# Mixture-of-experts stage of a two-layer trunk: first two narrow expert blocks taken whole, with twelve weight loads queued ahead of the register loads

## Chip, core and metric

The kernel runs on one core of a Trainium2 chip. The metric is the device time of one execution in microseconds, smaller is better; the time of a kernel is the median of its runs.

## What is computed

The reference is a two-layer trunk on 256 tokens of width 1024. Each layer adds a mixing block (a recurrent group, an attention group and a gated group) and a feed-forward block. The feed-forward block is dense in layer 0 and a top-2-of-8 mixture of experts in layer 1. The change lies in this last part:

```
def moe_swiglu(h, router, wg, wu, wd):          # h: (1, 256, 1024) float32
    t = h.reshape(256, 1024)
    logits = (t @ router).astype(float32)         # 8 experts
    top_v, top_i = lax.top_k(logits, 2)
    gates = softmax(top_v)
    gate_full = sum(one_hot(top_i, 8) * gates[..., None], axis=1)
    out = 0
    for e in range(8):                            # wg, wu: 1024x3584, wd: 3584x1024 each
        out = out + gate_full[:, e:e+1] * ((silu(t @ wg[e]) * (t @ wu[e])) @ wd[e])
    return out
```

The weights of the eight experts are 8 x 42 pieces of 1 MB in float32, 336 loads in all, and every one of them is read.

## The kernel before

**Places.** The kernel serves the experts in eight places. Place 0 is always expert 0, whose number is known when the program is built; the other seven are filled by the number of tokens, and their expert numbers are worked out on the chip (tile `order`) and read into registers of the DMA-issuing engine SP. Places 1, 2 and 3 are WIDE (128 token columns; place 1 carries a QUARTER piece of 32 more), places 4 to 6 are NARROW (64) and places 0 and 7 are QUARTER (32). For every place the tokens are gathered by matmuls with a one-hot matrix (`prepare`, L1250 for the narrow places, L1264 for the wide ones), evacuated by ACT and DVE into `xgs` or `xg`.

**Blocks.** An expert is worked in 7 blocks of 512 hidden columns. A block takes 6 loads: j = 0 to 3 (gate and up weights) and j = 4, 5 (down weights). A narrow block multiplies the float32 weights as they are: `small_up` (L1486 for a QUARTER, L1470 for a NARROW), then a transpose (L1510, copied by ACT at L1513) and `small_down` (L1539). A wide block first splits every half of a load into a high part (`wh`, ACT, L196) and a low part (`wl`, DVE, L197) and uses three matmuls for each product (L201 to L203); at place 1 the same loads then serve `quarter_up` (L1486), which is the last reader of j = 0 to 3.

**What sets the order.** `work` goes through the wide blocks. In every turn it does the up part of one wide block, the down part of the wide block before, the down parts of the narrow blocks taken up in the turn before, and the up parts of two more (or one). Before its first turn it does `small_up` of the first LEAD = 2 narrow blocks, both of expert 0. `halves` hands out the loads in that order, `take` pulls one half and refills the queue `feed` with `fill` (window of 10 halves, 3 of them split). The order on each engine is then set by a scheduler when the program is built; `tc.issue_after(i)` puts an instruction behind `i` on the engine of `i`.

**Buffers.** Expert loads go in a ring of 12 buffers of 1 MB: 8 of pool `raw2` and 4 of pool `raw`. Load n + 12 can be issued when the last reader of load n is done. Before the experts, `raw2` holds the work area of the mixing block and `raw` the last weights of that block (w_out).

**Number the loads from 0.** Before: 0 to 7 are j = 0 to 3 of the two lead blocks; 8 to 11 are j = 0 to 3 of the first wide block (place 1, so behind a register); 12 to 15 are j = 4, 5 of the lead blocks; 16 to 23 are j = 0 to 3 of the next two narrow blocks (expert 0 too); 24 to 27 the second wide block.

## Time and profile before

| | us |
|---|---|
| median of 3 runs (lowest to highest) | 1416.84 (1415.02 to 1419.85) |
| the profiled execution, its own time | 1414.25 |
| its span (first to last instruction) | 1412.50 |
| experts: from the first expert matmuls at 553.8 to the end | 859 |
| mean granted TensorE clock over the span, share of full speed | 0.97 |

The span is cut in stretches: layer 0 and the mixing block of layer 1 fill the first 540 us, the routing of the experts some 15 us behind them, and the experts the rest. In the last part TensorE and the DMA engines are both nearly always busy, so the busy shares alone don't say which of them sets the pace; the chain of waits does.

### The profile page before, as it was taken

The numbers are of one execution on the slowest core, as the hardware profiler recorded it, in microseconds if no ns is written. First come the engines' busy times: TensorE is split into PE (matmuls) and PEld (weight loads), VectorE is DVE, ScalarE is ACT, GpSimd is POOL, SyncE is SP. The second block draws the span as 40 slices with busy tenths as digits, with TensorE's granted clock in tenths as the row PEclk, the third lists the DMA queues.
The fourth block names the chain that finished last, engine by engine and source line by source line (L and its number), as shares of the span: only waits on it lengthen the run. The fifth ranks groups of instructions, "written<-read, shape, count | busy, mean of one in ns | idle before, by whom it ended". The sixth has DMA issues, their size and how long they took to land.

```text
span 1412.5 us, 24089 instructions
## 1 busy us (share of the span) xinstructions
PE 1330.2 (94%) x9860; PEld 965.4 (68%) x9860; DVE 715.0 (51%) x1052; ACT 629.0 (45%) x986; POOL 77.9 (6%) x127
## 2 busy tenths in 40 slices
PE   7989899999999898998999999999999999999986
PEld 7977678888888676765666555655766656656553
DVE  5686455445576555453335314524544446565443
ACT  7548264444575643453224313423434345444342
POOL 1250000000114111000000000000000000000000
PEclk9989999999999997999999999999999999999989
DMA  7410245555452231899999999989999999999995
GB/s 285 178 61 2 90 153 185 189 188 179 159 185 74 84 159 71 337 425 425 425 427 425 426 385 374 426 372 426 402 426 413 420 427 426 426 411 426 427 426 226
DMA packets 60438, 422.64 MB, mean 299 GB/s; under 512 B 7200, under 2 KB 8224, under 8 KB 10400
## 3 DMA queue, kind: packets, MB, share of 16 engines
q1 hardware_dynamic: 59760, 420.03, 73.1%
q8 instruction: 79, 1.29, 0.3%
q10 hardware_dynamic: 560, 1.00, 0.2%
q14 instruction: 39, 0.32, 0.1%
HBM read 419.95 MB, written 1.05 MB: 298 GB/s over the span
## 4 chain that ended last, share of the span: by engine, by line
PE 76%; DMA 10%; DVE 6%; ACT 3%; POOL 2%; issue 2%; SPq 0%; ACTq 0%; DVEq 0%; POOLq 0%
PE pb L1470 10%; DMA raw<-moe 10%; PE pb L202 8%; PE pb L201 7%; PE pb L203 7%; PE pa L1539 7%; PE pa L202 6%; PE pa L201 6%; PE pa L203 6%; PE pb L1486 4%; DVE wl L197 2%; PE pb L1250 1%; PE pa L371 1%; PE pa L373 1%; PE pa L372 1%
## 5 line engine op out<-in xcount | busy, mean ns | idle before, releaser
L197 DVE TENSOR_TENSOR wl<-raw,wh 128x1024 fp32r<-128x1024 f32 (+1 forms) x370 | 440.8, 1221 | 180.1 <-ACT wh L196 179.4
L196 ACT ACTIVATE wh<-raw 128x1024 fp32r<-128x1024 f32 (+1 forms) x370 | 380.5, 1053 | 230.8 <-PE pb L203 118.4
L202 PE MATMUL pb<-wl,xg 128*128 128x512 f32 x336 | 141.3, 420 | 13.2 <-DVE wl L197 12.4
L1470 PE MATMUL pb<-raw,xgs 128*64 128x256 f32 x1344 | 151.0, 380 | 0.0
L201 PE MATMUL pb<-wh,xg 128*128 128x512 f32 x336 | 136.7, 409 | 9.9 <-ACT wh L196 9.9
L203 PE MATMUL pb<-wh,xg 128*128 128x512 f32 x336 | 134.0, 399 | 0.0
L1470 PEld LDWEIGHTS pb<-raw,xgs 128*64 128x64 f32 x1344 | 95.0, 137 | 54.7 <-issue 9.3
L1539 PE MATMUL pa<-raw,aT 128*32 128x256 f32 (+1 forms) x1008 | 120.1, 454 | 0.0
L1486 PE MATMUL pb<-raw,xgs 128*32 128x256 f32 x1344 | 93.1, 395 | 10.1 <-DMA raw<-moe 10.1
L202 PEld LDWEIGHTS pb<-wl,xg 128*128 128x128 f32 x336 | 64.4, 192 | 41.9 <-DVE wl L197 25.9
L1473 ACT ACTIVATE a<-pb,rg 128x256 f32<-128x256 f32 x21 | 9.9, 473 | 174.9 <-PE pb L1470 174.9
L1501 DVE TENSOR_TENSOR aT<-pb,aT 128x512 fp32r<-128x512 f32 x21 | 14.5, 692 | 143.7 <-ACT aT L1500 143.7
L201 PEld LDWEIGHTS pb<-wh,xg 128*128 128x128 f32 x336 | 64.2, 191 | 32.1 <-ACT wh L196 18.2
L1539 PEld LDWEIGHTS pa<-raw,aT 128*32 128x32 f32 (+1 forms) x1008 | 42.8, 118 | 61.9 <-issue 46.2
L1486 PEld LDWEIGHTS pb<-raw,xgs 128*32 128x32 f32 x1344 | 45.2, 113 | 50.9 <-DMA raw<-moe 14.1
L202 PE MATMUL pb<-wl,hTh 128*128 128x512 f32 (+1 forms) x192 | 73.0, 380 | 0.0
L203 PEld LDWEIGHTS pb<-wh,xg 128*128 128x128 f32 x336 | 64.5, 192 | 12.1
L203 PE MATMUL pb<-wh,hTl 128*128 128x512 f32 (+1 forms) x192 | 71.6, 377 | 0.0
L202 PE MATMUL pa<-wl,aT 128*128 128x512 f32 x168 | 69.0, 411 | 0.5 <-DVE wl L197 0.5
L201 PE MATMUL pb<-wh,hTh 128*128 128x512 f32 (+1 forms) x192 | 67.5, 378 | 0.7 <-ACT hTh L284 0.7
L203 PE MATMUL pa<-wh,aT 128*128 128x512 f32 x168 | 66.5, 396 | 0.0
L1475 DVE SCALAR_TENSOR_TENSOR a<-pb,rg,a 128x256 f32<-128x256 f32 x21 | 10.2, 484 | 99.4 <-PE pb L1470 99.4
(384 smaller groups left out, 2058.0 us busy)
## 6 DMA issues: line engine op xcount, KB each, us to landing
raw<-moe SPq DMA_DIRECT2D x336, 1024.0 KB, 12.3
raw<-wst SPq DMA_DIRECT2D x54, 1024.0 KB, 4.8
raw<-wst SPq DMA_DIRECT2D x4, 832.0 KB, 5.1
area<-sw_in SPq DMA_DIRECT2D x2, 960.0 KB, 7.1
area<-sw_in SPq DMA_DIRECT2D x2, 664.0 KB, 6.2
x<-x_in SPq DMA_DIRECT2D x2, 512.0 KB, 5.1
raw<-wst SPq DMA_DIRECT2D x2, 512.0 KB, 7.0
out_dram<-x SPq DMA_DIRECT2D x8, 128.0 KB, 2.7
```

The costliest lines, as they stand in the source:

```text
L196: act(h[:, 0:n], t[:, a:b], AF.Copy)
L197: (E or V).tensor_tensor(lo[:, 0:n], t[:, a:b], h[:, 0:n].bitcast(F32), op=ALU.subtract)
L201: T.matmul(o, lhsT=xh, rhs=wh, start=first, stop=False)
L202: T.matmul(o, lhsT=xh, rhs=wl, start=False, stop=False)
L203: T.matmul(o, lhsT=xl, rhs=wh, start=False, stop=last)
L371: T.matmul(ps, lhsT=wh[:, s_], rhs=hTh[:, k, :], start=(k == 0), stop=False)
L372: T.matmul(ps, lhsT=wh[:, s_], rhs=hTl[:, k, :], start=False, stop=False)
L373: T.matmul(ps, lhsT=wl[:, s_], rhs=hTh[:, k, :], start=False, stop=(k == KD - 1))
L1470: T.matmul(ps[HALF[hv], :], lhsT=z[:, k, :], rhs=w[:, o_:o_ + 256], start=(k == 0), stop=(k == KD - 1))
L1486: T.matmul(ps[QUART[g], :], lhsT=z[:, k, :], rhs=ws[g // 2 * 4 + k // 2][:, o_:o_ + 256], start=(k == 0), stop=(k == KD - 1))
L1501: V.tensor_tensor(z[:, :, 1, :], p3, z[:, :, 0, :].bitcast(F32), op=ALU.subtract)
L1539: T.matmul(acc[rows, :], lhsT=aT[:, f, :], rhs=ws[f][:, g * w:g * w + w], start=(i == 0 and f == 0), stop=(i == NB - 1 and f == 3))
```

## The change

- The order in which the loads are handed out: all six loads of the two lead blocks come first (j = 0 to 3 of both, then j = 4, 5 of both), and twelve loads instead of ten halves are queued before the first register is needed. While this stock lasts, `take` refills nothing.
- The two lead blocks are done whole, up and down, before the first wide turn; their `small_down` is taken out of the first turn.
- The first six splits of the first wide block are put behind the copies of the transposed activations of the two lead blocks (`last_a`) and behind the last gather copy of the wide place (`gathered`).
- The low part `xl` of the gathered input is made by DVE for both token tiles, behind the choice of the experts (`chosen`); before, GpSimd made one of them. Both copies `xh` go behind the last `xT` copy.

```diff
         for t in range(2):
             V.tensor_tensor(xn[:, t, :], x[:, t, :], gr, op=ALU.mult)
-            held_a = act(xh[:, t, :], xn[:, t, :], AF.Copy)
+            with tc.issue_after(last_T.ins):
+                held_a = act(xh[:, t, :], xn[:, t, :], AF.Copy)
...
-        V.tensor_tensor(sel, best[:, :, 0, :], best[:, :, 1, :], op=ALU.add)
-        for t, E in enumerate((V, G)):
-            E.tensor_tensor(xl[:, t, :], xn[:, t, :], xh[:, t, :].bitcast(F32), op=ALU.subtract)
+        chosen = V.tensor_tensor(sel, best[:, :, 0, :], best[:, :, 1, :], op=ALU.add)
+        with tc.issue_after(chosen.ins):
+            for t in range(2):
+                V.tensor_tensor(xl[:, t, :], xn[:, t, :], xh[:, t, :].bitcast(F32), op=ALU.subtract)
...
-                        yield *(split(r_, a_, b_, h2_p, l2_p) if own else split(r_, a_, b_)), r_[:, a_:b_]
+                        with ExitStack() as held:
+                            for i_ in last_a if cnt_splits[0] <= 6 else ():
+                                held.enter_context(tc.issue_after(i_.ins))
+                            wh_, wl_ = split(r_, a_, b_, h2_p, l2_p) if own else split(r_, a_, b_)
+                        yield wh_, wl_, r_[:, a_:b_]
 
         def halves():
-            m, before = LEAD, narrows[:LEAD]
-            for b in before:
-                yield from units(*b, range(4))
+            m, before = LEAD, []
+            for js in (range(4), (4, 5)):
+                for b in narrows[:LEAD]:
+                    yield from units(*b, js)
...
             h = feed.popleft()
-            fill(-1)
+            if lead:
+                lead.pop()
+            else:
+                fill(-1)
             return h
...
         def work():
-            m, wjob = LEAD, None
-            before = [(np_, ni, small_up(np_)) for np_, ni in narrows[:LEAD]]
+            m, before, wjob = LEAD, [], None
+            blocks = [(np_, ni, small_up(np_)) for np_, ni in narrows[:LEAD]]
+            aTs = [small_T(a_, KINDS[np_][0], NARROW) for np_, _, a_ in blocks]
+            small_downs(blocks, aTs)
             drain()
+            last_a.append(gathered[0])
+            fill(0)
             ask(NARROWS[1])
...
         with tc.issue_after(held_v.ins), tc.issue_after(held_a.ins):
-            fill(0)
+            fill(0, 12 * LEAD)
+        lead = [None] * (12 * LEAD)
```

`small_downs` is the loop over `small_down` that stood in `work` before.

**SP, at the start of the experts.** The queue of the engine that issues the loads, from the last weights of w_out on; L1114 is a load of expert 0, L1116 one whose expert stands in a register, TENSOR_LOAD reads a register. Before:

```order
L189 DMA raw<-wst 128x2048 x4
L1114 DMA raw<-moe 128x2048 x8
L1178 TENSOR_LOAD order
L1178 ISA x2
L1116 ISA
L1116 DMA raw<-moe 128x2048
```

And now, the end of the register loads (seven of `order` stand behind the twelve loads) and what follows them:

```order
L189 DMA raw<-wst 128x2048 x4
L1114 DMA raw<-moe 128x2048 x12
L1180 TENSOR_LOAD order
L1180 ISA x2
...
L1612 TENSOR_LOAD flag_i
L1612 ISA x2
L1116 ISA
L1116 DMA raw<-moe 128x2048
```

Four more loads of expert 0 stand ahead of the first register load, and the loads of the first wide block behind all eight register loads, which came between them before.

**TensorE, from the lead blocks to the gathers of the first wide place.** L1486 (L1496 in the changed kernel) is `small_up`, L1264 (L1266) the gathers of the wide place. Before:

```order
L1215 MATMUL pb<-cc,pe 128x128 x2
L1486 MATMUL pb<-raw,xgs 32x256
L1217 MATMUL pb<-gsp,pe 128x2 x2
L1486 MATMUL pb<-raw,xgs 32x256 x63
L1264 MATMUL pb<-pe,xh 128x160 x2
L1264 MATMUL pb<-pe,xl 128x160 x2
```

And now, with L1520 the transposes and L1550 `small_down`:

```order
L1219 MATMUL pb<-gsp,pe 128x2 x2
L1496 MATMUL pb<-raw,xgs 32x256 x63
L1520 MATMUL pb<-cc,a 128x64 x2
L1550 MATMUL pa<-raw,aT 32x256 x16
L1520 MATMUL pb<-cc,a 128x64 x2
L1266 MATMUL pb<-pe,xh 128x160 x2
L1266 MATMUL pb<-pe,xl 128x160 x2
```

The transposes and down parts of both lead blocks come ahead of the first wide block (those of the second among the gathers, six rows further on); before, they stood behind its `quarter_up`.

**ACT, around the first splits.** L196 is the high part of a split, L1271 and L1274 copy the gathers of the wide place. Before:

```order
L1327 ACTIVATE e_5274<-e_5274,rq_y 128x2 x2
L1254 ACTIVATE xgs<-pb 128x4x32
L196 ACTIVATE wh<-raw 128x1024 x2
L1254 ACTIVATE xgs<-pb 128x4x32
L1219 ACTIVATE pT<-pb 128x256
L196 ACTIVATE wh<-raw 128x1024 x2
```

And now, behind the last of eight pairs of gather copies:

```order
L1271 ACTIVATE xg<-pb 128x256
L1274 ACTIVATE xgs<-pb 128x32
L196 ACTIVATE wh<-raw 128x1024 x4
L1221 ACTIVATE pT<-pb 128x256 x2
L1256 ACTIVATE xgs<-pb 128x256
L196 ACTIVATE wh<-raw 128x1024 x3
```

The four splits that were done during the lead blocks now follow the last gather copy.

## Rows read from the trace of the kernel before

**Rows 1.** Page, part 2: GB/s moved in 40 slices of 35.3 us.
```profile
GB/s 285 178 61 2 90 153 185 189 188 179 159 185 74 84 159 71 337 425 425 425 427 425 426 385 374 426 372 426 402 426 413 420 427 426 426 411 426 427 426 226
```
**Rows 2.** Chain of waits, experts: start, us, what (DMA: from issue to landing).
```profile
596.91 11.36 DMA raw<-moe
...
641.70 13.14 DMA raw<-moe
654.92 1.06 ACT wh L196
...
1273.57 15.88 DMA raw<-moe
...
1368.05 19.51 DMA raw<-moe
```
**Rows 3.** Windows: busy us by engine, granted clock, DMA share, GB/s.
```profile
520.00:555.00 35.00, 28.95 (x183) 22.68 (x181) 18.87 (x39) 11.62 (x23) 5.00 (x6) 0.91 0.01 1
555.00:560.00 5.00, 5.00 (x25) 5.00 (x25) 3.71 (x24) 0.28 (x1) 0.00 (x0) 0.50 0.28 79
590.00:595.00 5.00, 5.00 (x63) 3.41 (x65) 1.81 (x7) 0.38 (x1) 0.00 (x0) 1.00 0.08 31
610.00:615.00 5.00, 3.34 (x23) 2.96 (x20) 3.54 (x4) 4.25 (x5) 0.00 (x0) 0.86 1.02 431
615.00:620.00 5.00, 5.00 (x19) 3.96 (x18) 3.45 (x4) 3.57 (x6) 0.00 (x0) 0.80 1.01 423
```
**Rows 4.** Timeline of SP's DMA issues: start, us, line, count.
```profile
557.34 2.74 SPq L1116 DMA_DIRECT2D raw<-moe  x4
566.84 6.03 SPq L1114 DMA_DIRECT2D raw<-moe  x8
...
594.41 2.91 SPq L1114 DMA_DIRECT2D raw<-moe  x4
```
**Rows 5.** Timeline of TensorE: start, us, line, tile, count.
```profile
571.93 0.45 PE L1264 MATMUL pb<-pe,xh 128*128 128x160 f32 x2
...
575.57 0.54 PE L1204 MATMUL pb<-rip,pe 128*128 128x2 f32 x4
...
576.90 0.48 PE L201 MATMUL pb<-wh,xg 128*128 128x512 f32 x1
...
591.89 0.40 PE L202 MATMUL pb<-wl,xg 128*128 128x512 f32 x1
592.13 0.39 PE L203 MATMUL pb<-wh,xg 128*128 128x512 f32 x1
592.45 3.66 PE L1486 MATMUL pb<-raw,xgs 128*32 128x256 f32 x64
596.04 0.46 PE L1510 MATMUL pb<-cc,a 64*128 64x64 f32 x4
...
598.44 3.59 PE L1539 MATMUL pa<-raw,aT 128*32 128x256 f32 x60
...
611.90 0.50 PE L201 MATMUL pb<-wh,xg 128*128 128x512 f32 x1 [1.66 <-ACT wh L196]
```
**Rows 6.** Timeline of a transpose of a lead-sized block and its copy by ACT.
```profile
1392.53 0.33 PE L1510 MATMUL pb<-cc,a 64*128 64x64 f32 x2
1392.90 0.28 ACT L1513 ACTIVATE aT<-pb 128x128 f32<-128x128 f32 x1 [0.72 <-PE pb L1510]
```
**Rows 7.** Timeline of DVE: last split of w_out, choice of the experts.
```profile
534.83 1.23 DVE L197 TENSOR_TENSOR wl<-raw,wh 128x1024 fp32r<-128x1024 f32 x1
...
549.78 1.42 DVE L1325 TENSOR_TENSOR e<-mx 128x4 f32<-128x4 f32 x1
...
553.25 0.17 DVE L1168 SCALAR_TENSOR_TENSOR slot_e<-pb,sel 128x16 f32<-128x16 f32 x1 [1.54 <-PE pb L1165]
```
**Rows 8.** Timeline of GpSimd at the same place.
```profile
548.83 2.35 POOL L1160 TENSOR_TENSOR xl<-xn,xh 128x1024 fp32r<-128x1024 f32 x1 [14.77 <-ACT xh L1151]
```

More of the change, by code (lines that the diff above doesn't have):

```diff
@@ L1129, in experts @@
                         P(1, "ffng")[:, :, None].to_broadcast([128, KD, NE]), op=ALU.mult)
+        xl = big.tile([128, 2, DM], F32R, name="xl", tag="xl")
         xT = big.tile([128, 2, KD, 128], F32, name="xT", tag="xg", bufs=2)
@@ L1132, in experts @@
         xh = big.tile([128, 2, DM], F32R, name="xh", tag="xh")
-        xl = big.tile([128, 2, DM], F32R, name="xl", tag="xl")
         mx = sml("mx", [128, 2, 8])
@@ L1142, in experts @@
                     T.transpose(ps[:, k * 128:(k + 1) * 128], x[:, t, ks], ident)
-                act(xT[:, t, 4 * g:4 * g + 4, :], ps.rearrange("p (k s) -> p k s", k=4), AF.Copy)
+                last_T = act(xT[:, t, 4 * g:4 * g + 4, :], ps.rearrange("p (k s) -> p k s", k=4), AF.Copy)
                 for k in range(4 * g, 4 * g + 4):
@@ L1224, in scatter_parts @@
             res.append((pT, sg))
-        anchor = [None]
+        anchor, gathered = [None], [None]
         def prepare(p, xg, sc):
@@ L1268, in prepare @@
                     if kind == WIDE:
-                        act(tile_[:, k0:k0 + per], p4[:, :, :, o:o + w], AF.Copy)
+                        gathered[0] = act(tile_[:, k0:k0 + per], p4[:, :, :, o:o + w], AF.Copy)
                     else:
@@ L1418, in experts, with fill @@
         supply = halves()
-        def fill(n=0):
-            while len(feed) < WINDOW and sum(h[0] is not None for h in feed) <= AHEAD + n:
+        def fill(n=0, window=WINDOW):
+            while len(feed) < window and sum(h[0] is not None for h in feed) <= AHEAD + n:
                 h = next(supply, None)
@@ L1512, in small_T @@
                          bufs=2 if tag == NARROW else 1)[:, :, 0:w]
-            act(z.rearrange("p (h j) s -> p j h s", h=2), ps[:, 0:4 * w].rearrange("p (j h s) -> p j h s", j=2, h=2),
-                AF.Copy)
+            last_a[:] = [last_a[-1], act(z.rearrange("p (h j) s -> p j h s", h=2),
+                            ps[:, 0:4 * w].rearrange("p (j h s) -> p j h s", j=2, h=2), AF.Copy)]
             return z
         accs = {}
+        last_a = [None]
         def wide_down(p, i, aT):
@@ L1544, in ended, with small_downs @@
             (steps.append if final else steps.appendleft)(finish(ready[p][2][KINDS[p].index(kind)], acc, final))
+        def small_downs(blocks, aTs):
+            for (p, i, _), aT in zip(blocks, aTs):
+                kind = KINDS[p][0]
+                if i == 0:
+                    accs[p] = [pa()[:, 0:512 if kind == NARROW else 256]]
+                small_down(accs[p][0], kind, i, aT, [take()[2] for _ in range(4)])
+                if i == NB - 1:
+                    ended(p, kind, accs[p], p == NARROWS[-1])
         def work():
-            m, wjob = LEAD, None
-            before = [(np_, ni, small_up(np_)) for np_, ni in narrows[:LEAD]]
+            m, before, wjob = LEAD, [], None
+            blocks = [(np_, ni, small_up(np_)) for np_, ni in narrows[:LEAD]]
+            aTs = [small_T(a_, KINDS[np_][0], NARROW) for np_, _, a_ in blocks]
+            small_downs(blocks, aTs)
             drain()
+            last_a.append(gathered[0])
+            fill(0)
             ask(NARROWS[1])
@@ L1575, in work @@
                             ended(p, QUARTER, [accs[p, QUARTER]])
-                for (np_, ni, _), z in zip(before, nT):
-                    kind = KINDS[np_][0]
-                    if ni == 0:
-                        accs[np_] = [pa()[:, 0:512 if kind == NARROW else 256]]
-                    small_down(accs[np_][0], kind, ni, z, [take()[2] for _ in range(4)])
-                    if ni == NB - 1:
-                        ended(np_, kind, accs[np_], np_ == NARROWS[-1])
+                small_downs(before, nT)
                 new = narrows[m:m + TURNS[n]] if n < len(wides) else []
```

## The prediction, made before the changed kernel was run

> **What bounds the kernel now.** I read the traffic of the DMA engines over the span first [rows 1]. Until about 565 us they move 2 to 285 GB/s, then 337 in one slice, and from 600 us to the last slice 372 to 427. The experts' 336 loads of 1.049 MB (1024 KB) at 426 GB/s take 2.46 us each, 827 us in all, so most of the 859 us of this part is covered by loads alone. Then the chain of waits [rows 2], which says who sets the pace. There are three stretches. From 596.91 to 654.92 it hangs on loads: two pieces of DMA, 11.36 and 13.14 us, and behind the second the split of the first half of the third wide block (load 42, issued at 641.70). From 654.92 to 1273.57 no DMA piece stands in it: TensorE and its splits set the pace. From 1273.57 on it is DMA again, six pieces up to 1387.56, and a tail. TensorE's stretch begins when load 42 lands, and the last stretch begins where TensorE's ends. So whatever moves the landing of load 42 moves the end by as much, as long as the work behind it stays the same, which the order on the engines shows to be nearly so. The question is what the change does to load 42.
>
> The windows show two gaps of the loads ahead of it [rows 3]. From 520 to 555 the DMA engines move 1 GB/s: eight loads are down and the ninth stands behind a register; SP issues it at 557.34 [rows 4]. And from 590 to 595 they move 31 GB/s: load 20 needs the buffer of load 8, a weight of the first wide block, which is free only when `quarter_up` has read it. SP issues load 20 at 594.41 [rows 4], in the middle of `quarter_up`, which begins at 592.45 [rows 5]. From load 20 to load 42 there is no gap (the DMA share is 1.00 or more in every window of 5 us from 600 to 655, as in the two shown). Issue to first byte takes 1.7 us: the issue at 557.34 [rows 4] is followed by 79 GB/s over 555 to 560 [rows 3], which is 0.93 us of full flow, so it began at 559.07. By that, load 20 flows from 596.1 and load 24 from 596.1 + 4 x 2.46 = 605.9.
>
> **Part 1, twelve loads ahead of the registers.** In the gap of 35 us loads 8 to 11 (j = 4, 5 of the lead blocks) now flow too. Their buffers held w_out, whose last split ends at 536.06 [rows 7], and 1.7 us and four loads later, by 548, they are down. (At the worst they start at 557, as loads 8 to 11 do now, and the credit is nothing.) The order of loads from number 16 on is the same. Four loads less are left for later: **4 x 2.46 = 9.8 us of credit**.
>
> **Part 2, what the credit is good for.** The ring has 12 buffers, so load 12 waits for load 0, and that is read by the first lead block at about 566: the issue at 566.84 [rows 4] is this release today. Loads 12 to 23 then flow from about 568 to 568 + 12 x 2.46 = 597.5, their buffers being freed by the lead blocks in time. Load 24 needs the buffer of load 12, now the first weight of the first wide block, so it waits for the middle of the same `quarter_up` as load 20 today. Thus load 24 goes when load 20 went, plus the delay of `quarter_up`. The delay is what the change puts ahead of it on TensorE:
> - Down parts of two lead blocks: 64 records of L1539, 60 of them in 3.59 us [rows 5], **3.8**.
> - Four transposes, 596.04 to the next matmul at 596.43 (0.46 long, overlapping) [rows 5], **0.4**.
> - The wait for the first transposed activations: transpose at 1392.53, ACT's copy ends at 1393.18 [rows 6], of which TensorE works 0.2, **0.5**. The copy of the second block is hidden by 12 gathers that stand ahead of its down part (32 of them take the 3.64 us from 571.93 to 575.57 [rows 5], 12 take 1.4).
> - Four more changes of the matmul's shape: L203 to L1486 takes 0.32 from start to start against 0.24 between two wide ones [rows 5], **0.4** at the most.
> - The first split, now behind the last gather copy: a copy ends some 0.5 us behind the last gather, the split takes 1.06 [rows 2], and meanwhile TensorE has the 1.33 us from L1204 to the first L201 [rows 5], **0.25**. The low part (1.23 [rows 7]) is covered by the gathers of the next place, 16 of which now stand between the first L201 and L202. If that cover were gone the price is the rival of the splits below.
> - The start of the gathers, part 3: **-0.35**.
>
> Sum **5.0 us**, so `quarter_up` begins at about 597.4 and load 24 is issued at 599.4. Credit minus delay is 9.8 - 5.0 = **4.8 us**. The ring asks once more: load 36 needs load 24 read by the `quarter_up` of the second wide block, and would flow 4.8 us earlier. Today this block starts at 611.90, behind a load that lands at 608.27 [rows 2, 5]. New, `quarter_up` of the first ends at 601.1, the next two narrow blocks need 3.66 each, to 608.4, and the block starts at about 608.9 without a wait, 3.0 earlier; the windows of low clock that fall in it today (1.7 us, below) are the rest. If the clock falls there again, about 3 us are left: the lower bound of the main case is 2.5. The upper bound is 6.5, where shape changes, the split and the wait cost nothing.
>
> **Part 3, the choice of the experts.** `xl` of the second tile goes from GpSimd (2.35 us) [rows 8] to DVE (a subtraction of this shape takes 1.23 there) [rows 7]. L1325 is a subtraction of four columns, and it takes 1.42 us, up to 551.20, while GpSimd's `xl` ends at 551.18: it waits for that [rows 7, 8]. Without GpSimd's operation I give it 0.17, as `slot_e`, and `sel` is there 1.2 us earlier. But both `xl` (2.4 us together, overlapping a little) now stand on DVE between `sel` and `slot_e`, which today starts at 553.25 behind a wait of 1.54 us for matmuls. New: `sel` done at 550.5, `xl` to 552.9, `slot_e` at 552.9, 0.35 earlier, and with it the gathers of the lead blocks. The Trainium skill, SBUF — State Buffer, "Who interferes with whom", has it that a VectorE instruction with two inputs in SBUF is blocked by a GpSimd instruction that reads SBUF until that one is done. The trace agrees with its 1.42 us; if the stall stayed for another reason, the gain would be 3.6 instead of 4.8. The eight register loads in a row cost nothing: today six of them end between 560.08 and 566.84 [rows 4], so one takes 1.13 us at most; eight from 556.5 or so end by 566, when the first lead buffer is freed, and there are 2 us more between 597.5 and load 24's issue.
>
> **The sum.** Span 1412.50 - 4.8 = 1407.7, the execution's own time 1414.25 - 4.8 = 1409.45. The median of the runs is 2.59 above that execution, so 1416.84 - 4.8 = **1412.0**.
>
> **The rivals.**
> - *The credit is kept whole.* If `quarter_up` is no later, load 24 flows when load 20 did: 1416.84 - 9.8 = **1407.0**. For it: 0.5 us here and there of my terms overlap. Against: 3.8 us of down parts are real work ahead of `quarter_up`.
> - *TensorE falls to half clock among the new short waits.* Behind the wait for the load of 608.27 today's clock is 0.86 and 0.80 over two windows of 5 us [rows 3], which is 3.4 us at 1.2 instead of 2.4 GHz, 1.7 us lost. The lead blocks run at half clock until about 566 already. Two such losses ahead of `quarter_up` cost 3.4: gain 1.4, **1415.4**. The Trainium skill, TensorE: Matmul & The Clock Gate, "HAM oscillation — how this bites in real kernels", describes bursts that start cold after each wait for data; the windows of 610 to 620 agree. For: a wait for ACT and four shape changes in 10 us. Against: each is 0.5 us or less, and the one before 611.90 is 1.66 [rows 5].
> - *The splits fall behind; slower.* Four halves are split ahead today, none then. If in the first wide block each half waits for ACT and DVE in turn, 1.06 + 1.23 [rows 2, 7], instead of six matmuls 0.24 apart (1.44), a half costs 0.85 more, the block 6.8: **1418.8**. If the lead isn't won back in the second wide block, it is 13.6: **1425.6**. It decides from 4.8 us on, 0.6 a half. Against: DVE alone needs 1.23 for a half, less than TensorE's 1.44, so it can run ahead; and the gathers are between.
>
> That the change doesn't do what it says is out: the order shows the twelve loads first.
>
> **Chances.** Main case 60 (37 of it past 4.25 us, which is 0.3%, about what a measurement can tell from no change; 23 within), whole credit 13, clock 17 (within), splits 10 (half within, half slower). So faster 0.50, same 0.45, slower 0.05. The range takes in the main case, the whole credit and the clock, with a little above for the lower bound of both: 1407 to 1418; the splits are left out.
>
> **What would show it.** After: no gap at 520 to 535 in the DMA windows and twelve loads down before 557; a gap of about 3 us before load 24; `quarter_up` at about 597 instead of 592.45; the piece of DMA that ends in the split of the third wide block at 650 instead of 654.92; the same length from there to the end. If `quarter_up` comes past 602 the forecast is wrong, and if load 42 comes 5 us earlier and the end doesn't, the second stretch isn't as independent as I take it.

## The result and the profile after

| | before | after |
|---|---|---|
| median, first set of runs (6 of each kernel, side by side) | 1415.93 us | 1409.57 us (1405.66 to 1413.73) |
| ratio, 95% interval | | 0.9947 (0.9923 to 0.9970) |
| median, second set of runs (17 and 12) | 1416.44 us | 1411.31 us (1406.68 to 1420.35) |
| ratio, 95% interval | | 0.9965 (0.9942 to 0.9988) |
| span of the profiled execution | 1412.5 | 1409.0 |

The change makes the kernel faster by 6.4 us in the first set and by 5.1 us in the second; 4.8 was forecast. Both medians of after, 1409.57 and 1411.31, lie within the forecast range of 1407 to 1418, and the forecast itself was 1412.0.

The spans can't be set against each other as they are. The compute instructions ahead of the experts are the same in both, but they ran 2.4 us longer in the execution of after. The last update of `x` (L452 on VectorE), where the experts can begin, started at 543.64 before and at 546.05 after. Below I count from this start where I compare kernels: the **time from x**. From x to the end it is 868.86 before and 862.95 after, 5.91 less.

Where the time is saved shows in three views. First the windows, which answer [rows 3] (busy us of PE, PEld, DVE, ACT and POOL with instructions, granted clock, DMA share, GB/s):

```profile
525.00:530.00 5.00, 5.00 (x53) 3.96 (x53) 2.69 (x3) 2.12 (x2) 0.00 (x0) 1.00 0.50 179
530.00:535.00 5.00, 5.00 (x31) 3.57 (x30) 0.67 (x2) 0.86 (x2) 0.15 (x1) 1.00 0.43 180
...
600.00:605.00 5.00, 5.00 (x96) 3.03 (x100) 1.24 (x2) 0.47 (x1) 0.00 (x0) 1.00 0.53 151
605.00:610.00 5.00, 5.00 (x100) 3.02 (x96) 2.04 (x2) 2.47 (x3) 0.00 (x0) 1.00 1.01 419
610.00:615.00 5.00, 5.00 (x34) 3.71 (x23) 3.90 (x6) 4.19 (x7) 0.00 (x0) 1.00 1.00 424
615.00:620.00 5.00, 5.00 (x32) 4.38 (x31) 3.86 (x4) 4.09 (x7) 0.00 (x0) 1.00 1.02 429
...
655.00:660.00 5.00, 5.00 (x23) 4.01 (x23) 4.77 (x5) 3.84 (x4) 0.00 (x0) 1.00 1.01 423
```

Loads now flow between 525 and 535, where there were none. The second gap, 31 GB/s at 590 to 595 before, has moved behind 600 and is shorter: DMA share 0.53, so 2.4 us of this window are empty (about 3 were forecast). And the clock stays at 1.00 from 610 to 620, where it was 0.86 and 0.80.

Then the queue of the loads on SP, answering [rows 4] (start, us, line, count):

```profile
568.78 2.63 SPq L1116 DMA_DIRECT2D raw<-moe  x4
572.23 10.88 SPq L1114 DMA_DIRECT2D raw<-moe  x8
601.87 4.36 SPq L1116 DMA_DIRECT2D raw<-moe  x6
```

Load 12 goes out at 568.78 (22.73 from x), loads 16 to 23 up to 583.11, and load 24 at 601.87 (55.82 from x). Forecast was 599.4 by the clock of before, which is 55.8 from x.

Then TensorE, answering [rows 5]:

```profile
574.85 1.93 PE L1550 MATMUL pa<-raw,aT 128*32 128x256 f32 x32 [0.65 <-ACT aT L1523]
...
578.47 1.93 PE L1550 MATMUL pa<-raw,aT 128*32 128x256 f32 x32
...
584.30 0.50 PE L201 MATMUL pb<-wh,xg 128*128 128x512 f32 x1 [0.20 <-ACT wh L196]
...
599.91 10.57 PE L1496 MATMUL pb<-raw,xgs 128*32 128x256 f32 x192
```

The two down parts take 1.93 us each and stand among the gathers. The wide block starts at 584.30, and `quarter_up`, the first 64 records of the last row, at 599.91: 53.86 from x, 48.81 before.

Last ACT at the third wide block, answering the split at 654.92 in [rows 2]:

```profile
651.87 0.47 ACT L1498 ACTIVATE a<-pb,rg 64x256 f32<-64x256 f32 x1 [4.00 <-PE pb L1496]
652.37 2.00 ACT L196 ACTIVATE wh<-raw 128x1024 fp32r<-128x1024 f32 x2
654.81 2.01 ACT L196 ACTIVATE wh<-raw 128x1024 fp32r<-128x1024 f32 x2 [0.43 <-DMA raw<-moe]
```

Load 42 is split at 652.37, 106.32 from x. Before it was 111.28: 4.96 earlier. In after this split stands right behind a `silu` of a narrow block, so its start alone doesn't show the landing; by the trace load 42, issued at 640.07, takes 12.22 us and lands at 652.29, 106.24 from x, and before it landed at 641.70 + 13.14 = 654.84 [rows 2], 111.20 from x. That is 4.96 too.

**A ruler for the rest.** In every wide block ACT makes one `silu` of the first 512 columns (L1451 before, L1461 after). Its 21 starts, counted from x, are marks along the whole stretch that the granted clock ahead of x can't move. Each kernel's marks minus those of the first profile of after, in us (mark 1 is the second wide block, mark 2 the third, "end" the last instruction):

```
kernel             mark 0   mark 1   mark 2   mark 5  mark 10  mark 16     end
before              -5.29     4.64     6.51     6.04     6.02     6.21    5.91
after, 2nd profile   3.18     3.18     3.14     2.83     2.84     2.80    2.68
late four           -0.01     0.02     0.10     0.67     0.87     3.39    2.78
more delay           9.91     9.91    12.52    11.89    11.17    13.73   13.54
order alone         -3.58    16.71    17.66    16.93    17.15    19.69   18.96
order, forced       -5.08     8.65    10.04    10.43    11.15    11.10   11.95
xl alone            -5.78     4.92     7.32     6.89     6.98     7.47    6.97
splits free          3.44     3.68     3.72     5.16     5.18     5.17    5.37
third up first       3.05     2.52    -0.25    -1.35    -1.32    -1.33   -1.48
held                 0.00     0.00     0.17    -1.36    -2.79    -5.06   -2.77
third and held       3.05     2.50    -3.01    -2.33    -3.70    -5.92   -3.32
filled               3.54     3.55     3.59     5.74     5.73     5.70    6.70
```

The row of before reads: its first wide block stood 5.3 us earlier, its second 4.6 later, and from the third on it is 4.7 to 6.5 behind, nearly to the end. The row below it shows how far two executions of one program can lie apart.

### The profile page after: what moved, and what is told of

The parts are those of the page before. It is cut to its first block, busy times and chain, and to the rows that moved or that the text cites. A ratio compares the mean times of both kernels' runs of the same rounds, so it can differ in the third digit from the quotient of the medians.

```text
span 1409.0 us, 24079 instructions
## 1 busy us (share of the span) xinstructions
PE 1330.4 (94%) x9860; PEld 966.7 (69%) x9860; DVE 714.6 (51%) x1053; ACT 628.3 (45%) x986; POOL 77.3 (5%) x126
## 5 line engine op out<-in xcount | busy, mean ns | idle before, releaser
L196 ACT ACTIVATE wh<-raw 128x1024 fp32r<-128x1024 f32 (+1 forms) x370 | 379.9, 1053 | 224.1 <-PE pb L203 113.2
L201 PE MATMUL pb<-wh,xg 128*128 128x512 f32 x336 | 135.5, 406 | 7.8 <-ACT wh L196 7.8
L1550 PE MATMUL pa<-raw,aT 128*32 128x256 f32 (+1 forms) x1008 | 120.7, 454 | 0.6 <-ACT aT L1523 0.6
L1496 PE MATMUL pb<-raw,xgs 128*32 128x256 f32 x1344 | 93.0, 402 | 9.5 <-DMA raw<-moe 9.4
L1550 PEld LDWEIGHTS pa<-raw,aT 128*32 128x32 f32 (+1 forms) x1008 | 42.3, 118 | 63.6 <-issue 49.0
L201 PEld LDWEIGHTS pb<-wh,xg 128*128 128x128 f32 x336 | 63.8, 190 | 29.6 <-ACT wh L196 15.3
L1496 PEld LDWEIGHTS pb<-raw,xgs 128*32 128x32 f32 x1344 | 46.1, 115 | 50.2 <-issue 14.0
L201 PE MATMUL pb<-wh,hTh 128*128 128x512 f32 (+1 forms) x192 | 67.4, 377 | 0.7 <-ACT hTh L284 0.7
```

What stands on the lines that cost most here:

```text
L196: act(h[:, 0:n], t[:, a:b], AF.Copy)
L201: T.matmul(o, lhsT=xh, rhs=wh, start=first, stop=False)
L1496: T.matmul(ps[QUART[g], :], lhsT=z[:, k, :], rhs=ws[g // 2 * 4 + k // 2][:, o_:o_ + 256], start=(k == 0), stop=(k == KD - 1))
L1550: T.matmul(acc[rows, :], lhsT=aT[:, f, :], rhs=ws[f][:, g * w:g * w + w], start=(i == 0 and f == 0), stop=(i == NB - 1 and f == 3))
```

## The experiments

**1. Is it the gap of 35 us?** Part 1 of the prediction said that four loads are gained because they flow in the gap ahead of the registers. Here the loads 8 to 11 go back behind a register.

```diff
-                r_ = eload(ready[p][0], 6 * i + j)
+                late = (p, i) in narrows[:LEAD] and j > 3
+                r_ = eload(late_e[0] if late else ready[p][0], 6 * i + j)
...
+            late_e.append(nc.values_load(order[0:1, 0:1], engines=[mybir.EngineType.SP], min_val=0, max_val=NE - 1))
...
-            fill(0, 12 * LEAD)
+            fill(0, 8 * LEAD)
```

> Loads 8 to 11 (j = 4, 5 of the lead blocks) stand behind a register load again, as loads 8 to 11 did before the change; their expert, still expert 0, is read from the first entry of order. All else is the changed kernel: the blocks are whole, and the order of the loads is the same. Theory A, part 1 of the prediction: the gain comes from four loads that flow in the gap of 35 us. Then it is lost here, 9.8 us: 1409.6 + 9.8 = 1419.4, and no less than 1416. Theory B, the ring: from about 557 to 568 the DMA engines have nothing else that they may do, since load 12 waits for load 0, which the first lead block reads at about 566 in either kernel. Then loads 8 to 11 flow in that hole, load 12 goes out when it does in the changed kernel (568.8), and the time is that of the changed kernel, 1409.6 within 2 us. What gains by B is only which load stands at number 8 to 11: one that a lead block reads, and not one that waits for quarter_up.

Measured: 1412.44 us beside 1417.65, ratio 0.9973 (0.9953 to 0.9993). SP's queue:

```profile
555.86 11.51 SPq L1116 DMA_DIRECT2D raw<-moe  x8
568.15 11.79 SPq L1114 DMA_DIRECT2D raw<-moe  x8
597.80 4.36 SPq L1116 DMA_DIRECT2D raw<-moe  x6
```

Loads 8 to 11, the first four of the first row, go out from 555.86 on, as late as before the change. Yet load 16 goes out 26.18 from x here and 26.18 in after, load 24 55.83 here and 55.82 in after, and the marks are the same to 0.1 us up to the third wide block. **Theory A falls.** Some 1 to 3 us come on much later, at marks 9 to 16. A few gathers and splits stand in another order in this program; that they cost it is not shown. The ratio's interval overlaps that of after.

**2. Does the end follow load 24 one for one?** The lead down parts are done two times more.

```diff
-                small_down(accs[p][0], kind, i, aT, [take()[2] for _ in range(4)])
+                ws = [take()[2] for _ in range(4)]
+                for _ in range(2 if (p, i) in narrows[:LEAD] else 0):
+                    ps = pb()[:, 0:256]
+                    for f in range(4):
+                        for g, rows in enumerate(QUART):
+                            T.matmul(ps[rows, :], lhsT=aT[:, f, :], rhs=ws[f][:, g * 256:g * 256 + 256],
+                                     start=(f == 0), stop=(f == 3))
+                small_down(accs[p][0], kind, i, aT, ws)
```

> The changed kernel with every matmul of the two lead down parts done two times more into a spare accumulator that nobody reads: 128 more records, 7.7 us at 1.93 us for 32, ahead of quarter_up of the first wide block. Theory A (the prediction's second step, one for one): quarter_up and load 24 come 7.7 us later, the gap before load 24 grows from 3.7 to 11.4 us, load 42 and the end come 7.7 us later: 1409.6 + 7.7 = 1417.3. Rival: the work behind load 42 isn't tied to it, or some of the delay is taken up by the wait of TensorE of 3.1 us at 645 to 655: the end moves by 4.6 us or less, 1414.2 or below.

Measured: 1422.68 us beside 1417.65, ratio 1.0029 (1.0010 to 1.0048), so some 11 us behind after. Load 24 goes out at 65.74 from x, 9.9 later and not 7.7. The 128 records took 7.11 us, and the first wide block starts at 590.91, 45.00 from x, where in after it was 38.25: 6.75 later. The other 3.2 us are the granted clock, which fell in the first wide block:

```profile
590.00:595.00 5.00, 4.80 (x28) 4.52 (x27) 4.46 (x9) 4.53 (x7) 0.00 (x0) 0.70 1.01 423
595.00:600.00 5.00, 5.00 (x16) 3.91 (x15) 2.28 (x6) 2.07 (x2) 0.00 (x0) 0.62 0.99 416
```

A clock of 0.70 and 0.62 over 5 us each is 3.4 us of work lost (0.30 and 0.38 of 5). The 9.91 at mark 1 is 11.2 to 13.7 from mark 2 to the end. What comes on top at mark 2 is a second fall, 0.86, 0.50 and 0.95 over 660 to 675, where after had 1.00. None of the delay of load 24 is taken up on the way: load 42 lands 9.7 later, and the rival is out.

**3. The order of the loads without the whole blocks.** The twelve loads stay ahead, the down parts go back behind `quarter_up`.

```diff
-            aTs = [small_T(a_, KINDS[np_][0], NARROW) for np_, _, a_ in blocks]
-            small_downs(blocks, aTs)
+            kept = [[take()[2] for _ in range(4)] for _ in blocks]
...
+                if n == 0:
+                    small_downs(blocks, [small_T(a_, KINDS[np_][0], NARROW) for np_, _, a_ in blocks], kept)
```

> Only the order of the loads is changed: twelve loads ahead of the registers, but the transposes and down parts of the lead blocks stay behind quarter_up of the first wide block, as before the change. quarter_up is then not delayed. Rival (the credit alone counts): 1407 or less. Theory B (the ring): load 20 needs the buffer of load 8, which is now read by the first lead down part, behind quarter_up and the transposes, some 2 us after it. So load 20 goes out at about 601 by the changed kernel's clock of events, where there load 24 goes at 601.9; four loads, 9.8 us, more are left behind the gap: 1409.6 + 9 = 1418.6, slower than the kernel before.

Measured: 1427.69 us beside 1417.65, ratio 1.0078 (1.0052 to 1.0105). By the marks it is 15 to 20 us behind after, where 9 were expected. The scheduler had put the four loads of the fourth narrow block behind six others, and TensorE stood for them:

```profile
618.10 1.07 PE L1499 MATMUL pb<-raw,xgs 128*32 128x256 f32 x4 [12.70 <-DMA raw<-moe]
```

So this run doesn't measure the ring alone. In the next one the order of the queue is held (each load of 17 to 41 by `tc.issue_after` behind the one before it).

> As the order alone (twelve loads ahead, down parts of the lead blocks behind quarter_up), but with loads 16 to 41 held in the order of the changed kernel on their queue; in the run before this the scheduler had put the four loads of the fourth narrow block behind six others. By the ring, load 20 goes out when the first lead down part has read load 8: quarter_up ended at 53.9 behind the last update of x there, transposes and down part take some 2.8, so 56.7; it flows at 58.4, load 24 at 68.2, against 57.5 in the changed kernel (load 24 issued at 55.8): 10.7 us later. The marks from the second wide block on then lie about 10 us behind the changed kernel's and 5 behind the kernel before's. If the credit of part 1 were a matter of the gap ahead of the registers alone, they would lie ahead of the changed kernel's.

Measured: 1424.19 us beside 1418.98, ratio 1.0037 (1.0008 to 1.0067). The windows show the gap:

```profile
590.00:595.00 5.00, 5.00 (x54) 3.50 (x56) 1.80 (x7) 0.55 (x2) 0.00 (x0) 1.00 0.00 0
595.00:600.00 5.00, 5.00 (x94) 2.94 (x90) 0.49 (x1) 0.91 (x3) 0.00 (x0) 1.00 0.01 3
600.00:605.00 5.00, 4.30 (x80) 2.61 (x72) 0.13 (x1) 0.47 (x1) 0.00 (x0) 1.00 0.73 242
```

Load 20 begins to flow at about 601.4 (a share of 0.73 of the last window is 3.6 us), 57.0 from x; 58.4 was expected. Load 24 lands at 71.90 from x by the trace, in after at 60.74: 11.2 later, and 10.7 was expected. The marks are 8.7 to 11.2 behind after's, and the time is 5.2 longer than before's. With the blocks cut in two, the order that has the credit by part 1 is slower than no change at all. So the gain is made by both together: the loads 8 to 11 must be of a kind that is read before `quarter_up`.

**4. Part 3 alone**, in the kernel before (`xl` on VectorE behind `chosen`, `xh` behind `last_T`, as in the diff ahead of the prediction).

> The kernel before with part 3 of the change alone: both xl on VectorE behind the choice, xh behind the last xT; loads and blocks as before. Measured from the last update of x (543.64 before, 546.05 after), so that the part ahead of the experts drops out. Theory (part 3): the subtraction of four columns falls from 1.42 to some 0.15 us, and slot_e and the gathers are 0.35 to 0.9 earlier; load 20, which waits for quarter_up, and all behind it come earlier by that, so the first marks of the wide blocks move by -0.35 to -0.9 against the kernel before (changed kernel: -4.6 at the second wide block). Rival: this part carries most of the gain; then the marks move by -3 or more.

Measured in one run: mark 0 is 0.49 earlier than before's, mark 1 is 0.28 later, and the end 1.1 later (1418.19 us beside 1418.98). Load 24 goes out 0.48 earlier (54.27 from x, before 54.75). So the first step is as expected, but it isn't handed on: this part alone gains nothing that shows in this run. Why it isn't handed on stays open.

**5. The hold of the splits.** The first six splits go where the scheduler puts them.

```diff
-                            for i_ in last_a if cnt_splits[0] <= 6 else ():
+                            for i_ in ():
```

> The changed kernel without the hold on the first six splits. On ACT the first splits, of loads 12 and 13, then stand among the copies of the two transposed activations. Load 12 goes out at 568.8 and can't land before 573, so the second silu and the first copy (574.0 and 574.5 in the changed kernel) wait for the two splits of load 12, some 1.6 us, and the second copy likewise. Theory (a short wait on ACT is passed on to TensorE): the first down part starts 1 to 1.6 us later and, less the 0.25 that the first split no longer costs behind the gathers, quarter_up and load 24 come 0.8 to 1.4 us later. Rival (the hold costs more than it gives): the early splits let the first wide block run faster, and quarter_up comes 0.25 us or more earlier.

Measured in one run, 1422.70 us, of which some 9 us more than before's are in the stretch ahead of x; ACT (start, us, line):

```profile
581.04 2.00 ACT L196 ACTIVATE wh<-raw 128x1024 fp32r<-128x1024 f32 x2 [3.49 <-DMA raw<-moe]
583.07 0.47 ACT L1498 ACTIVATE a<-pb,rg 64x256 f32<-64x256 f32 x1
583.56 0.28 ACT L1523 ACTIVATE aT<-pb 128x128 f32<-128x128 f32 x1
583.78 2.00 ACT L196 ACTIVATE wh<-raw 128x1024 fp32r<-128x1024 f32 x2
587.54 0.28 ACT L1523 ACTIVATE aT<-pb 128x128 f32<-128x128 f32 x1 [1.76 <-PE pb L1520]
```

ACT stands 3.49 us for load 12, and the second `silu` and the first copy wait behind it. From x (552.58 here) the `silu` is at 30.5 instead of 28.0, the second copy at 35.0 instead of 31.0, and load 24 goes out 3.7 later. The direction is right, but 0.8 to 1.4 was expected; up to 1.7 us of the 3.7 is the clock, at 0.94 and 0.72 over 580 to 590, and even without them it is more. The end is 5.4 behind after, about as much as the whole change gained; but the 1.4 between marks 2 and 5 come with another fall, 0.91 over 700 to 720. What the missing hold itself costs at load 24 is thus between 2.0 and 3.7 in this one run, and another run may differ.

**6. The same kernel again.**

> The changed kernel once more, on the chip and beside the runs of before that the next kernel has, and a second profile of it. Where all that counts is set by the program, the marks of the wide blocks, measured from the last update of x, come out as in the first profile within 0.3 us up to the sixth, and what differs later by 1 to 2 us is the granted clock. The time: 0.9947 of the kernel before, within 0.002.

The ratio, 0.9965, is within what was expected, the marks are not: 3.18 later from the first on. The first wide block starts at 581.83, 38.26 from x, where it started at 38.25 in the first profile. Right behind that:

```profile
580.00:585.00 5.00, 4.81 (x33) 4.67 (x32) 4.14 (x12) 5.00 (x10) 0.00 (x0) 0.78 1.02 429
585.00:590.00 5.00, 5.00 (x14) 3.92 (x14) 3.21 (x7) 1.66 (x4) 0.00 (x0) 0.53 1.00 423
```

The clock fell in the first wide block: 0.22 and 0.47 of 5 us, 3.4 us lost, ahead of `quarter_up`. That is the prediction's second rival, in its place and at its price. It comes in some executions of one and the same program. Its reason isn't borne out: the first profile has the same short waits of 0.65 and 0.20 us and no fall. In the same place, just behind the start of the first wide block, the clock fell in experiment 2 and in experiment 7 below, and it stayed up in experiments 1 and 8.

**7. Is it the waits that bring the clock down?** Two matmuls of 512 columns that nobody reads are put into the waits of TensorE in the choice of the experts.

```diff
+        def idle(i):
+            with tc.issue_after(i.ins):
+                return T.matmul(pb(), lhsT=ident, rhs=cc[:, 0:512], start=True, stop=True)
+
+        idle(last_r)
...
-        T.matmul(ps[:, NE:2 * NE], lhsT=C("ones"), rhs=sel[:, 0, :], start=False, stop=True)
+        idle(T.matmul(ps[:, NE:2 * NE], lhsT=C("ones"), rhs=sel[:, 0, :], start=False, stop=True))
```

> The changed kernel with two matmuls of 512 columns that nobody reads, one in each wait of TensorE in the choice of the experts (1.19 us ahead of L1165, 1.33 us ahead of the first gather). In every profile so far TensorE's granted clock falls to half there, at about 551, and comes back at about 568; the gathers and the first lead block run at half. Theory (the waits bring the fall): with the waits filled the clock stays up, the gathers and the lead blocks, 13 us at half, take some 6 less, load 12 goes out up to 6 us earlier and the first mark comes 5 to 6 us earlier than in the changed kernel. Rival (it falls all the same, for the short matmuls of 8 and 32 columns that make up this stretch): the marks stay, or come up to 1 us later for what the two cost beyond the waits.

Measured: 1414.72 us beside 1418.36, ratio 0.9965 (0.9938 to 0.9992), no better than after.

```profile
550.00:555.00 5.00, 4.92 (x40) 4.35 (x38) 3.97 (x7) 2.23 (x4) 0.00 (x0) 1.00 0.01 3
555.00:560.00 5.00, 5.00 (x18) 3.72 (x18) 3.35 (x10) 3.30 (x9) 1.47 (x2) 0.51 0.00 0
```

The clock has two levels here, 1.00 and 0.50 of full speed (2.4 and 1.2 GHz). A mean of 0.51 over the second window puts the fall at 555.1, 4.4 us from x, behind 5 us in which TensorE was busy for 4.92. The first of the two matmuls starts at 556.34, so the clock was down by then: it fell among the matmuls of 8 columns (L1145) that stand ahead of it. The first profile of after fits that: its clock of 0.61 over 550 to 555 is a fall at 551.1, and L1145 ends at 551.34, where the first of the two waits only begins. Read this way, the fall comes 4.4 to 5.2 us from x in every one of the thirteen profiles. So these waits don't bring the clock down, and filling them is too late. The theory falls. What does bring it down stays open: the matmuls of 8 columns stand there in every kernel, and further ahead, from 540 to 550, TensorE was idle for 3.0 us in this run; neither was changed here. The marks come 3.5 later: the first gather 0.54 later, 1.7 us by another fall at 590 to 600 (0.77 and 0.89), and the rest by the clock's later return.

**8. Closing the gap that is left.** If the ring is what counts, the third narrow block's up part ahead of the wide block frees the buffer that load 24 waits for.

```diff
-TURNS = [2] * 7 + [2, 1, 1, 2, 1, 2, 1] + [1, 1, 2, 1, 1, 2, 1]
+TURNS = [1] + [2] * 6 + [2, 1, 1, 2, 1, 2, 1] + [1, 1, 2, 1, 1, 2, 1]
...
+            before = narrows[m:m + 1]
+            m += 1
+            yield from units(*before[0], range(4))
             for n in range(len(wides) + 1):
...
             fill(0)
+            before = [(np_, ni, small_up(np_)) for np_, ni in narrows[m:m + 1]]
+            m += 1
```

> The changed kernel with small_up of the third narrow block (place 0 again) ahead of the first wide block, its loads as 12 to 15 and those of the wide block as 16 to 19; its down part follows in the first turn. Theory B (the ring): load 24 then needs a buffer that the third block's up part has read by 588, so there is no gap before it; load 28 needs quarter_up, which is done by 606, and would flow at 609.9: no gap either. Load 42 lands 3.6 us earlier. TensorE waits for 3.1 us between 645 and 655 in the changed kernel, so it can gain no more than that: 1409.6 - 3.1 = 1406.5. Rival: the wait for a buffer only moves on to a later load, or the longer stay ahead of quarter_up delays the second wide block: 1409.6 or more.

Measured: 1409.32 us beside 1417.65, ratio 0.9935 (0.9911 to 0.9958). The gap is gone: from 575 on no window of 5 us has a DMA share under 0.99 up to 700. But the marks come 1.3 earlier and not 3.1. At the third wide block TensorE waits as long as before, for another reason:

```profile
651.61 0.47 ACT L1501 ACTIVATE a<-pb,rg 64x256 f32<-64x256 f32 x1 [3.09 <-PE pb L1499]
652.11 4.89 ACT L196 ACTIVATE wh<-raw 128x1024 fp32r<-128x1024 f32 x5
```

Five splits run without a pause, so their loads lie there. They stand behind the `silu` of the narrow block, which waits for TensorE. TensorE waits for a split at nearly every wide block of after; its waits from 600 us on (us in total, times, longest):

```profile
PE pb L202 <- DVE wl L197: 12.0, 15, 1.3
PE pb L1496 <- DMA raw<-moe: 9.4, 6, 3.7
PE pb L201 <- ACT wh L196: 7.6, 5, 1.7
```

So two more versions hold `silu` and product of the narrow block ahead of a wide one behind the last split handed out, one on after and one on the version with the third up part.

```diff
-            act(a[HALF[1], :], ps[HALF[0], :], AF.Silu, scale=rs[-1][HALF[0], :])
+            with behind(hold, 0):
+                act(a[HALF[1], :], ps[HALF[0], :], AF.Silu, scale=rs[-1][HALF[0], :])
...
+        def behind(hold, k):
+            return tc.issue_after(last_s[k].ins) if hold else ExitStack()
...
-                    before.append((np_, ni, small_up(np_)))
+                    before.append((np_, ni, small_up(np_, (np_, ni) == new[-1] and n + 1 < len(wides))))
```

> The changed kernel with one more edit: in the last narrow block ahead of each wide block, silu is held on ACT behind the last split that has been handed out, and the product behind it on VectorE behind the low part of that split. In the changed kernel TensorE waits 0.3 to 2.4 us at the head of nearly every wide block for a split that stands behind these two; 19.6 us in all. Theory C: between 655 and 1273 TensorE sets the pace, so what these waits take there (about 12 us) is won, until the loads set the pace, whose queue has some 14 us to spare in that stretch (the slices at 368 to 420 GB/s): the end comes 5 to 12 us earlier, 1398 to 1405. Rival: the last stretch hangs on loads, and these are issued when buffers come free by work that stays where it is: 1409 within 2.

> Both edits on top of the changed kernel: the up part of the third narrow block ahead of the first wide block, and silu and product of the narrow block ahead of a wide one held behind the splits. Apart they moved the marks in the middle by -1.3 and by up to -7.3, and the end by -1.5 and -2.8. Theory (the last stretch hangs on loads, and what is won ahead of it counts only as far as loads are issued earlier): the marks in the middle come 3 to 8 earlier than the changed kernel's, the end 3 to 4.5: 1405 to 1407 on the scale of 1416 for the kernel before. Rival: the first wait, at the third wide block, was what kept the first edit small; then both add up to more, 1404 or less.

Measured: held 1408.65 us beside 1418.98, ratio 0.9934 (0.9903 to 0.9964); both 1405.70 beside 1416.44, ratio 0.9924 (0.9896 to 0.9953), where after had 1411.31 beside the same runs of before. With both, the waits are

```profile
PE pb L1505 <- DMA raw<-moe: 12.9, 8, 3.7
PE pb L204 <- DVE wl L199: 6.5, 14, 0.8
PE pb L203 <- ACT wh L198: 2.9, 2, 1.7
```

and the marks come up to 8.1 earlier (mark 17, 7.3 by the hold alone), but the end only 3.3. The waits for splits fell from 19.6 to 9.4 us, those for loads rose from 9.4 to 12.9. The chain of waits shows where these stand. The last stretch hangs on loads, in after from

```profile
1323.83 19.49 DMA raw<-moe
1343.34 19.86 DMA raw<-moe
1363.31 19.78 DMA raw<-moe
1383.17 1.07 ACT wh L196
```

and with both edits, by their own clock, from much earlier on:

```profile
1265.26 17.94 DMA raw<-moe
1283.31 20.58 DMA raw<-moe
1304.02 19.44 DMA raw<-moe
1323.57 19.45 DMA raw<-moe
```

So part of TensorE's gain turns into waits for loads, as the theory of the last expectation has it. Where the chain passes to loads doesn't by itself tell the time, though: in before it does so at 1273.57 too. The version with both edits has the lowest time of all. That it beats after rests on one set of runs; the intervals of the two ratios overlap.

## Why the prediction was right, step by step

- **The bound.** Right. Load 42 came 4.96 earlier (its split at 652.37, which is 649.96 by the clock of before; 650 was forecast) and the end 5.9, with the marks between at 4.7 to 6.5. In before, both profiles of after and experiments 1 to 5 and 7, ten profiles in all, load 42 lands between 106.2 and 122.6 from x, and the end follows 756.3 to 760.6 behind it. What the second stretch adds to 4.96 is the clock: before ran the start of the third wide block at 0.79 and 0.86 (655 to 665), 1.75 us lost, after at 1.00:

```profile
655.00:660.00 5.00, 3.22 (x9) 2.33 (x10) 3.93 (x4) 4.50 (x6) 0.00 (x0) 0.79 1.02 429
660.00:665.00 5.00, 5.00 (x26) 3.72 (x28) 3.64 (x4) 2.52 (x3) 0.00 (x0) 0.86 1.02 426
```

  The second wide block starts 3.05 earlier (611.26, 65.21 from x, before 68.26; 3.0 was forecast).
- **Part 1.** The size of the credit was right, the reason wrong. I wrote that loads 8 to 11 now flow in the gap at 520 to 555, and that the credit is nothing if they start at 557. Experiment 1 starts them there and loses nothing up to the third wide block. Load 12 waits for load 0, which is read about 23 us from x in any of these kernels, and four loads nearly fit between the first register and that: load 12 lands 2.1 later in experiment 1 (29.81 from x, in after 27.67), and `quarter_up` doesn't wait for it. What the change gives is the place of the wait: the ring stops at the first load whose buffer a late reader holds, `quarter_up`. Before, that was load 20, since load 8 was of the wide block; now it is load 24. My own second part says just this ("load 24 goes when load 20 went, plus the delay"), and the sum was made with it. So the number came out right, but for part 1 taken alone that was luck.
- **Part 2, the delay.** 5.0 forecast, 5.05 measured (48.81 to 53.86 from x). Its terms: down parts 2 x 1.93 = 3.86 (3.8); wait for the first transposed activations 0.65 (0.5); wait for the first split 0.20 (0.25); from the first L201 to `quarter_up` 15.61, before 15.55, so the splits don't fall behind (third rival, out). What is left for the transposes and the changes of shape is 0.75 (0.8). The gathers start 0.91 earlier (0.35), but the clock comes back at 22.15 from x in both kernels, thus later against the work, and the lead up parts end only 0.5 earlier. That the two misses nearly cancel is luck.
- **The hold of the splits** stood in the sum as a cost of 0.25, and what it prevents stood nowhere. By experiment 5 the change without it issues load 24 3.7 later in that execution, up to 1.7 of it by the clock. That was a gap in the working: of an edit that holds something back, the price of not holding belongs in it too.
- **Part 3.** The subtraction of four columns took 1.42 [rows 7], ending when GpSimd's `xl` did [rows 8]. With that on VectorE it takes 0.14:

```profile
551.74 0.14 DVE L1327 TENSOR_TENSOR e<-mx 128x4 f32<-128x4 f32 x1
...
552.38 2.35 DVE L1162 TENSOR_TENSOR xl<-xn,xh 128x1024 fp32r<-128x1024 f32 x2
554.65 0.17 DVE L1170 SCALAR_TENSOR_TENSOR slot_e<-pb,sel 128x16 f32<-128x16 f32 x1
```

  This agrees with the rule of the Trainium skill, SBUF — State Buffer, "Who interferes with whom", that the prediction weighed. `slot_e` starts 8.60 from x, before 9.61 [rows 7]: 1.0 earlier, and 0.35 was forecast. `sel` comes 1.66 earlier (1.2 forecast), and the two `xl` that now stand ahead of `slot_e` take back 0.65 of it. Half of that reached the end of the lead up parts, for the clock came back no earlier. Alone, in the one run of experiment 4, this part gained nothing at the end.
- **The registers.** Load 12 goes out 22.73 from x, before load 12 went at 23.20: eight in a row cost nothing, as forecast. By the trace of after the eight reads follow each other 0.56 to 0.82 us apart and are done by 563.2; SP then stands for more than 5 us until load 0 has been read.
- **The clock.** In the first profile of after it stayed up ahead of `quarter_up`, in the second it fell, at the 3.4 us of the rival. I had given that 17%, as one outcome for the kernel. It is one of single executions, and the median lies over both. The Trainium skill, TensorE: Matmul & The Clock Gate, "Part 1: The HAM clock gate (the "warmup" mystery)", says of one kernel that it "measures 6, 11, or 14 cold-MMs depending on the HAM phase at kernel start" (matmuls at the lower clock). The two profiles of after agree in that the loss varies, 0 and 3.4 us in the same place of the same program; the reason that the page gives is not shown here. Of the fall at 610 to 620 in before, which the prediction read as a burst that starts cold behind a wait, the windows show something else: the burst starts at 611.90 at the full clock, and the fall comes at 613.6 (0.86 over 610 to 615).
- **The whole credit** (first rival) is out: the delay was there in full, and the gap before load 24 with it.
- **The sum.** 4.8 forecast, 6.4 and 5.1 measured; the second is closer to it, and both intervals hold it. From x to the end the two profiles of after are 5.9 and 3.2 shorter than that of before; the clock stayed at 1.00 from 570 to 705 in the first and fell in the second.

## What to carry to other kernels

In a ring of buffers, number the loads and write down the last reader of each: a load is only as early as the reader of the one that had its buffer, so let the loads that stand one ring ahead be those that are read first. An idle stretch of the DMA engines is worth something only if the next wait on a buffer moves too. And compare executions from the last event that the change can't touch, since the stretch ahead of it differs by more than the change is worth.

## What was not expected of the hardware

- The stretch ahead of x, the same compute instructions in all thirteen profiles, took 541.97 to 552.58 us. In the two longest (550.65 and 552.58) its mean granted clock was 0.94 and 0.95, in the others 0.96 or 0.97. The 2.4 us between before and after aren't explained by that: both had 0.96.
- Falls of the clock in the experts' part come in some executions and not in others, even of one program, and one costs a good part of what the change is worth: 1.7 us at 610 to 620 and 1.75 at 655 to 665 of before, none there in after, 3.4 at 580 to 590 of after's second profile, 3.4 at 590 to 600 of experiment 2.
- The clock can fall without a wait just ahead of it: in experiment 7 it fell behind 5 us with TensorE busy for 4.92 of them. The waits further ahead are not excluded.
